# Moving part of the modulation rows' products from VectorE to GpSimd and ScalarE in a two-layer diffusion trunk

## The chip, the cores and the metric

The kernel runs on one core of a Trainium2 chip. Five engines take part, each with its own instruction queue served in order: TensorE (PE in the profile, with PEld for its weight loads), VectorE (DVE), ScalarE (ACT), GpSimd (POOL) and SyncE (SP), from which nearly all transfers are issued. The metric is the device time of one execution in microseconds.

## The reference

The trunk has two layers over 640 tokens (128 of context, 512 latent) of width 2048, all in float32. A layer is a modulated RMS norm, a wide input projection into mixer branches, the mixers, a SiLU gate and an output projection with a gated residual:

```python
shift, scale, gate = modulation(c_ctx, ada_w[l], ada_b[l])     # silu(cond) @ w + b, split in 3
h = rms_norm(x, norm_g[l]) * (1.0 + scale) + shift
...                                                            # y = mixer(h) * silu(gate path)
x = x + gate * (y @ w_out[l])
```

Context tokens use `c_ctx`, latent tokens `c`; so every modulation vector exists twice, once per condition. Layer 0 mixes with windowed attention and gated linear attention (GLA), layer 1 with neighbourhood attention and a spatial-gating MLP. The part that matters here is `modulation`: for each of the 6144 outputs of a layer and each of the two conditions, a dot product over 2048 inputs. In the kernel most of these are not matrix products on TensorE, but products of weight rows with the condition row.

## The kernel before, in words

Features lie on partitions: the activations are 16 tiles of 128 features by 640 tokens. TensorE multiplies in three passes, each operand being split into a high and a low part (`whi`, `wlo` for weights, `acth`, `actl` for activations); ScalarE copies the high part of a weight unit (128 x 512 as a rule), GpSimd subtracts it to get the low part.

The whole order of work is written by a planner at build time. `Pace` keeps a clock for each engine (`t["v"]` VectorE, `t["a"]` ScalarE, `t["g"]` GpSimd), adds a modelled cost to it for each instruction, and knows when a tile will be ready; `self.now` is TensorE's clock. After a few matrix products `tick` is called: it lets the tasks of the main work go on (`tasks`), as long as VectorE and ScalarE are not over `cap` ahead of `now`, and then up to four steps of one low-priority task, `self.low`, but only while `t["v"]` is at most `now + room`. `rooms` gives this threshold: its first value from the end of the start to the second half of the attention (`spill_y`), its third from there, its second from `open_g0` on. `need(flag)` moves the planned clock on, without matrix products of the main line, until a flag is set. `until(tile)` lets a task wait until the plan has a tile ready.

The low-priority task is that of the modulation rows, `ada_task`. It runs three jobs in one chain: `b0` (6 tiles of 128 outputs, a correction of the first gate chunks by the shift), `g0` (16 tiles, layer 0's gate) and `1` (32 tiles, layer 1's shift and scale); later a fourth, `g1`, in narrower pieces. A job goes over the 2048 inputs in four quarters of `PIECE` = 512. At the beginning of a quarter it loads both condition rows, spread over all 128 partitions, and ScalarE copies them into PSUM banks 6 and 7. Then for each tile it loads a 128 x 512 piece of weights into one of four slots of `adas`, and VectorE forms two products with sum (`tensor_tensor_reduce`), one for each condition: a pair.

```python
acc = self.part[name][:, f + k, c : c + 1]
nc.vector.tensor_tensor_reduce(
    junk[:, : bank[c].shape[1]], raw[:, k, :], bank[c], 1.0, acc if q else 0.0, ALU.mult, ALU.add, acc
)
yield pace
```

Each such product is two records in the profile, `CUSTOM_DVE_ANT_0` and a read of the accumulator. The result of job `1` is awaited with `need("ada_1")` ahead of the handover to layer 1; shift and scale are formed from it by `fin_scale` and `shift1`.

The start (`start`) loads inputs, weights for layer 0's scale (24 tiles by TensorE, in `tiles`) and does six first chunks in windows, as activation tiles come in. Beside it runs `shifts` as the low task: the same kind of products for 8 tiles of layer 0's shift, in a ring of `NRAW` pieces. There the two condition rows are not loaded 128-fold: a load of 2 x 512 is split into `chi` and `clo`, and four matrix products with `one` spread them into PSUM banks 2 and 3, in each quarter.

After the start come the GLA heads, the attention heads, then `open_g0`, which is called when the last attention head is done (flag `ya7`): it closes the pool of `YB` and opens the buffers for layer 0's output and layer 1.

## Time and profile before

| what | value |
|---|---|
| median of three runs | 2125.49 us (2121.93 to 2128.29) |
| profiled execution | 2125.07 us |
| its span | 2123.3 us |
| TensorE busy | 2060.7 us (97%) |
| VectorE busy | 1385.2 us (65%) |
| ScalarE busy | 999.3 us (47%) |
| GpSimd busy | 1151.8 us (54%) |
| granted TensorE clock | 0.993 |

In the profile an instruction is named by its line (most have L213, where a helper records each operation, L386 for matrix products, L420 for loads), its engine, its operation, the tile it writes and those that it reads. `adas<-adas,bank,part` is a row product of job `1`, `partg` belongs to `g0` and `g1`, `partb` to `b0`, `raw` and `sh` to the products of the start. Of a group the count, the busy time and the mean of one in ns are given, then the idle time of the engine just ahead of it with what ended it. A view of windows gives busy microseconds of each engine in each stretch, with the granted clock, the share of busy transfer engines and GB/s at the end. A view of one tile gives minimum, median and maximum in ns, and the start of the first and of the last. A line of the waits gives the total, the count and the longest; a line of the timeline the start, the duration and, in brackets, the idle time before it.

### The profile page before, as it was taken

Reading aid. Unit: us, or ns where it says so; the run is one execution under the profiler, and the core shown is the slowest. Engines: PE = TensorE matmul, PEld = TensorE weight load, DVE = VectorE, ACT = ScalarE, POOL = GpSimd, SP = SyncE. Lnnn points to the kernel's source line nnn. Section 1 sums busy time; section 2 is a strip of 40 time slices with the busy share of each in tenths; the row PEclk is TensorE's granted clock in tenths of the full one; section 3 lists DMA queues with packets and bytes.
Section 4 is the critical chain, followed back from the end, with each engine's and each line's share of the span. In section 5 each row is a group of like instructions: output and inputs, shape, how many; then the busy total and the mean of one; then the engine's idle time right before and its main releaser. Section 6 shows DMA issues by size and latency. Waiting matters only on the chain. (4 is left out here: it accounts for less than half of the span.)

```text
span 2123.3 us, 40020 instructions
## 1 busy us (share of the span) xinstructions
PE 2060.7 (97%) x14361; PEld 2007.1 (95%) x14361; DVE 1385.2 (65%) x3260; ACT 999.3 (47%) x2244; POOL 1151.8 (54%) x969
## 2 busy tenths in 40 slices
PE   7999999998999999999999999999999999999996
PEld 6899999998999999999989999999999999999995
DVE  5868777777565664989766878787454444465335
ACT  4424464443555565543464434445444544454433
POOL 4423343333323333788565656555555577668882
PEclk9999999999999999999999999999999999999998
DMA  9956343335454444576734455444222344354327
GB/s 364 377 188 202 116 136 105 114 125 178 148 189 149 139 138 143 179 239 227 248 131 105 130 166 158 139 137 154 89 81 94 107 136 131 124 202 132 127 95 248
DMA packets 192263, 339.13 MB, mean 160 GB/s; under 512 B 20824, under 2 KB 70072, under 8 KB 192064
## 3 DMA queue, kind: packets, MB, share of 16 engines
q1 hardware_dynamic: 190592, 335.02, 47.6%
q8 instruction: 112, 1.84, 0.3%
q10 hardware_dynamic: 1472, 1.56, 0.2%
q14 instruction: 87, 0.71, 0.1%
HBM read 302.00 MB, written 31.88 MB: 157 GB/s over the span
## 5 line engine op out<-in xcount | busy, mean ns | idle before, releaser
L386 PE MATMUL bank<-acth,whi 128*128 128x320 f32 (+2 forms) x3320 | 1022.9, 319 | 18.0 <-ACT bc L213 5.4
L386 PE MATMUL bank<-actl,whi 128*128 128x320 f32 (+2 forms) x3320 | 995.9, 311 | 3.5 <-POOL actl L213 1.7
L386 PE MATMUL bank<-acth,wlo 128*128 128x320 f32 (+2 forms) x3320 | 995.7, 311 | 3.4 <-POOL wlo L213 3.3
L213 POOL TENSOR_TENSOR wlo<-wraw,whi 128x512 fp32r<-128x512 f32 (+1 forms) x452 | 576.2, 1287 | 626.1 <-ACT whi L213 561.4
L386 PEld LDWEIGHTS bank<-acth,whi 128*128 128x128 f32 (+1 forms) x3320 | 618.6, 189 | 28.5 <-ACT bc L213 6.2
L386 PEld LDWEIGHTS bank<-actl,whi 128*128 128x128 f32 (+1 forms) x3320 | 618.4, 189 | 7.1 <-POOL actl L213 2.7
L386 PEld LDWEIGHTS bank<-acth,wlo 128*128 128x128 f32 (+1 forms) x3320 | 618.5, 189 | 5.0 <-POOL wlo L213 5.0
L213 POOL TENSOR_TENSOR wlo<-rs,whi 128x384 fp32r<-128x384 f32 x370 | 406.1, 1117 | 179.5 <-ACT whi L213 143.2
L213 ACT ACTIVATE whi<-wraw 128x512 fp32r<-128x512 f32 (+1 forms) x460 | 263.5, 588 | 138.3 <-PE bank L386 80.6
L386 PE MATMUL bank<-eh,whi 128*128 128x322 f32 (+1 forms) x666 | 209.3, 314 | 0.3 <-ACT whi L213 0.3
L386 PE MATMUL bank<-eh,wlo 128*128 128x322 f32 (+1 forms) x666 | 207.1, 311 | 1.8 <-POOL wlo L213 1.8
L386 PE MATMUL bank<-el,whi 128*128 128x322 f32 (+1 forms) x666 | 206.9, 311 | 0.0
L213 ACT ACTIVATE whi<-rs 128x384 fp32r<-128x384 f32 x370 | 181.4, 514 | 47.1 <-PE bank L386 40.1
L213 DVE CUSTOM_DVE_ANT_0 adas<-adas,bank,partg 128x256 bf16<-128x256 f32 (+1 forms) x320 | 178.5, 558 | 14.4 <-DMA adas<-ada_g 6.4
L213 DVE TENSOR_TENSOR wraw<-rs 128x768 f32<-128x768 f32 x74 | 98.3, 1329 | 122.2 <-POOL wlo L213 51.7
L213 DVE CUSTOM_DVE_ANT_0 adas<-adas,bank,part 128x512 bf16<-128x512 f32 x192 | 143.0, 745 | 15.3 <-DMA adas<-ada 10.6
L213 ACT ACTIVATE arena<-arena,bc 128x512 f32<-128x512 f32 (+4 forms) x211 | 106.3, 528 | 90.3 <-DVE arena L213 87.3
L386 PEld LDWEIGHTS bank<-eh,wlo 128*128 128x128 f32 x666 | 125.5, 188 | 2.7 <-POOL wlo L213 2.5
L386 PEld LDWEIGHTS bank<-eh,whi 128*128 128x128 f32 x666 | 125.7, 189 | 0.6 <-ACT whi L213 0.6
L386 PEld LDWEIGHTS bank<-el,whi 128*128 128x128 f32 x666 | 125.8, 189 | 0.0
L213 POOL TENSOR_TENSOR arena<-arena 128x320 f32<-128x320 f32 (+1 forms) x66 | 70.6, 1069 | 76.5 <-ACT arena L213 65.7
L213 ACT ACTIVATE arena<-Y 128x320 f32<-128x320 f32 (+1 forms) x76 | 38.9, 512 | 151.3 <-DVE Y L213 128.1
(210 smaller groups left out, 2316.1 us busy)
## 6 DMA issues: line engine op xcount, KB each, us to landing
wraw<-w_even SPq DMA_DIRECT2D x176, 256.0 KB, 3.3
adas<-ada_g SPq DMA_DIRECT2D x128, 256.0 KB, 3.6
adas<-ada SPq DMA_DIRECT2D x128, 256.0 KB, 3.6
rs<-w_odd SPq DMA_DIRECT2D x50, 384.0 KB, 3.3
wraw<-w_odd SPq DMA_DIRECT2D x74, 256.0 KB, 3.4
wraw<-w_out SPq DMA_DIRECT2D x64, 256.0 KB, 3.8
rs<-w_odd SPq DMA_DIRECT2D x50, 256.0 KB, 3.6
Y<-ada SPq DMA_DIRECT2D x24, 512.0 KB, 7.1
```

Source lines behind the costliest of these rows:

```text
L213: return f(*args, **kw)
L386: self.nc.tensor.matmul(out, lhsT, rhs, start=start, stop=stop, **kw)
```

## The change

Three things change.

First, the products for the second condition (c = 1) may be taken off VectorE. `offload` gives one to GpSimd as a plain elementwise product into one of two buffers (`prods`), if fewer than two are open and GpSimd's planned clock is not past `now` (`mixed` is 0). `collect`, called ahead of each product, lets ScalarE sum a finished buffer into a column of `psum`. GpSimd reads the condition row from a copy in SBUF, `mixrow`. At the end of a job, VectorE adds the four quarters' columns to the job's result. From `open_g0` on `prods` is empty, and all products are VectorE's again. The same is done in the start.

Second, the first threshold `rooms[0]` goes from 0.3 to 0.0: from the start's end to `spill_y`, a step of the row task is taken only when VectorE's planned clock is not past `now`.

Third, in the start the condition rows come 128-fold by transfer, one row at a time, and ScalarE copies them into the banks; the split and the four matrix products per quarter go. The ring of pieces shrinks from six to five, and `junk` and `crow` move into free parts of `adas`.

```diff
+        self.mixrow = [self.t(yb, [128, PIECE], "mixrow", bufs=2) for _ in range(2)]
+        self.prods = [self.t(yb, [128, PIECE], "prod", bufs=2) for _ in range(2)]
+        self.made, self.nprod = [], 0
+        self.psum = self.P([128, 4, 32], "psum")
+        for x in self.part.values():
+            nc.gpsimd.memset(x, 0.0)
...
-    cap, hold = 2.0, 99.0
-    lags0, room0, rows_at, pace0, NRAW, NRING = (0.2,) * 5, 1.2, 20.0, 0.4, 6, 6
+    cap, hold, mixed = 2.0, 99.0, 0.0
+    lags0, room0, rows_at, pace0, NRAW, NRING = (0.2,) * 5, 1.2, 20.0, 0.4, 5, 6
-    rooms, calms, lags = (0.3, 1.5, 0.9), (3.0, 3.0), (3.0, 3.0, 2.0, 1.0, 0.4)
+    rooms, calms, lags = (0.0, 1.5, 0.9), (3.0, 3.0), (3.0, 3.0, 2.0, 1.0, 0.4)
...
     def ada_task(self, jobs):
...
-            if isinstance(job, list):
-                for k, b in enumerate(job):
+            if len(job) == 2:
+                for k, b in enumerate(job[0]):
                     nc.scalar.activation(b, raw[:, k, :], AF.Copy)
+                    if self.prods and b is self.banks[7]:
+                        nc.scalar.activation(self.mixrow[job[1] % 2], raw[:, k, :], AF.Copy)
+                        if job[1] == 0:
+                            nc.gpsimd.memset(self.psum, 0.0)
...
+                    self.collect()
+                    if c == m == 1 and self.offload(raw[:, 0, :], self.mixrow[q % 2], self.psum[:, q, f : f + 1]):
+                        yield
+                        continue
                     nc.vector.tensor_tensor_reduce(
-                        junk[:, : bank[c].shape[1]], raw[:, k, :], bank[c], 1.0, acc if q else 0.0, ALU.mult, ALU.add, acc
+                        junk[:, : bank[c].shape[1]], raw[:, k, :], bank[c], 1.0,
+                        acc if (f + k, c) in begun else 0.0, ALU.mult, ALU.add, acc
                     )
...
             if last:
+                while self.made:
+                    self.collect()
+                    yield
+                begun.clear()
+                if m == 1:
+                    for q in range(4):
+                        acc = self.part[name][:, :, 1]
+                        nc.vector.tensor_tensor(acc, acc, self.psum[:, q, 0 : acc.shape[1]], ALU.add)
...
+    def offload(self, raw, row, acc):
+        if len(self.made) >= len(self.prods) or self.pace.t["g"] > self.now + self.mixed:
+            return False
+        x = self.prods[self.nprod % len(self.prods)]
+        self.nprod += 1
+        self.nc.gpsimd.tensor_tensor(x, raw, row, ALU.mult)
+        self.made.append((x, acc))
+        return True
+
+    def collect(self, force=False):
+        while self.made and (force or self.left(self.made[0][0]) <= 0.0):
+            x, acc = self.made.pop(0)
+            self.nc.scalar.activation(x, x, AF.Copy, accum_out=acc)
...
             def shifts():
...
-                junk = self.t(su, [128, PIECE // 2], "junk").bitcast(BF16)
-                one = self.t(su, [2, 2, 128], "one", F32R)
-                hi, lo = (self.t(su, [2, PIECE], x, F32R) for x in ("chi", "clo"))
-                nc.vector.tensor_copy(one, self.ident[0:2, 0:2, None].to_broadcast([2, 2, 128]))
+                junk = self.adas[:, 1472 : 1472 + PIECE // 2].bitcast(BF16)
...
-                    todo += [(None, d["crow_s"][:, cs]), *((f, d["ada_s0"][f, :, cs]) for f in range(NB))]
+                    todo += [(-c, d["crow_s"][2 - c : 3 - c, cs].partition_broadcast(128)) for c in (2, 1)]
+                    todo += [(f, d["ada_s0"][f, :, cs]) for f in range(NB)]
...
-                    if f is None:
-                        raw = raw[0:2, :]
-                        yield from self.until(raw)
-                        nc.scalar.activation(hi, raw, AF.Copy)
-                        nc.vector.tensor_tensor(lo, raw, hi.bitcast(F32), ALU.subtract)
+                    if f < 0:
+                        nc.scalar.activation(pc[f + 2], raw, AF.Copy)
+                        if f == -1:
+                            nc.scalar.activation(self.mixrow[q % 2], raw, AF.Copy)
                         load(i + len(raws) - 1)
-                        yield from self.until(hi, lo)
-                        for c, p in enumerate(pc):
-                            self.mm(p, one[:, c, :], hi, stop=False)
-                            self.mm(p, one[:, c, :], lo, start=False)
                         continue
...
         def open_g0():
             self.need("ya7")
+            self.collect(True)
+            self.prods = []
```

In `shifts` the products get the same `collect` and `offload` calls, and the same four additions behind them.

## The prediction

> **What bounds the kernel now.** I read the page's first part first, to see which engine is full.

> ```profile
> span 2123.3 us, 40020 instructions
> PE 2060.7 (97%) x14361; PEld 2007.1 (95%) x14361; DVE 1385.2 (65%) x3260; ACT 999.3 (47%) x2244; POOL 1151.8 (54%) x969
> ```

> TensorE is the bound; it is idle for 2123.3 - 2060.7 = 62.6 us, and no work moved between the other three engines can gain more than the part of that idle time which the moved work causes. So I next asked for the busy time of each engine by stage, cut at 148 (the start ends), 228 and 533 (the loads of `ada_g0` and `ada_1` begin), 790 (the moved work is nearly over) and 1041 (the last row product of layer 1 ends).

> ```profile
> core 0: us, PE busy (x) PEld busy (x) DVE busy (x) ACT busy (x) POOL busy (x), PEclk, DMA share, GB/s
> 0.00:28.00 28.00, 17.81 (x216) 13.94 (x216) 7.67 (x14) 13.14 (x28) 11.66 (x16) 1.00 0.91 354
> 28.00:110.00 82.00, 75.27 (x926) 65.70 (x927) 67.98 (x139) 39.72 (x86) 38.93 (x27) 1.00 0.98 378
> 110.00:148.00 38.00, 38.00 (x276) 36.41 (x276) 29.68 (x81) 7.30 (x15) 10.64 (x10) 1.00 0.45 151
> 148.00:228.00 80.00, 80.00 (x547) 79.99 (x546) 61.76 (x127) 36.46 (x70) 31.52 (x25) 1.00 0.58 187
> 228.00:533.00 305.00, 296.31 (x2029) 291.16 (x2028) 220.52 (x432) 137.53 (x261) 120.08 (x80) 0.99 0.40 131
> 533.00:790.00 257.00, 254.63 (x1692) 244.53 (x1691) 157.20 (x479) 147.47 (x373) 84.07 (x64) 1.00 0.46 152
> 790.00:900.00 110.00, 107.50 (x718) 105.25 (x717) 75.18 (x156) 59.43 (x130) 61.23 (x49) 1.00 0.48 157
> 900.00:1041.00 141.00, 135.42 (x909) 133.99 (x908) 122.83 (x281) 53.28 (x120) 112.82 (x104) 0.99 0.69 231
> ```

> The second number is TensorE's busy time. From 148 to 790 it loses 11.1 us (8.7 + 2.4), from 790 to 1041 8.1 us, from 28 to 110 6.7 us, from 110 to 148 nothing. In 28 to 110 the DMA engines are at 0.98: that stage is fed by transfers. Now what ended the losses, by the waits of TensorE for 148 to 790:

> ```profile
> PE bank L386 <- ACT bc L213: 5.4, 3, 3.5
> PE bank L386 <- DVE arena L213: 2.5, 5, 1.1
> PE bank L391 <- ACT arena L213: 2.4, 3, 1.1
> PE bank L391 <- DVE Y L213: 0.8, 1, 0.8
> ```

> These are releases of PSUM banks by the evacuation: VectorE multiplies, ScalarE copies the bias columns after it. Row products sit in VectorE's queue between such steps. The clearest case is the last of them, in order of time:

> ```profile
> 1035.56 0.31 PE L386 MATMUL bank<-acth,whi 128*128 128x320 f32 x1
> 1036.14 0.75 DVE L213 CUSTOM_DVE_ANT_0 adas<-adas,bank,part 128x512 bf16<-128x512 f32 x1 [4.54 <-DMA adas<-ada]
> 1037.60 0.89 DVE L213 TENSOR_TENSOR bank<-bank,sums 128x320 f32<-128x320 f32 x2
> 1038.53 1.14 DVE L213 SCALAR_TENSOR_TENSOR Y<-bank,G,arena 128x128 f32<-128x128 f32 x3
> 1039.26 0.42 PE L386 MATMUL bank<-acth,whi 128*128 128x320 f32 x1 [3.39 <-DVE Y L213]
> ```

> VectorE stood 4.54 us for a piece of layer 1's rows, the evacuation stood behind it, and TensorE lost 3.39 us. The code has a `need("ada_1")` here; the rows were barely in time.

> **The change part by part.** Durations of what goes and comes, by form:

> ```profile
> L213 DVE CUSTOM_DVE_ANT_0 adas<-adas,bank,part 128x512 bf16<-128x512 f32 x192 | 143.0, 745 | 15.3 <-DMA adas<-ada 10.6
> L213 DVE DVE_READ_ACCUMULATOR2_ANT part<- 128x1 f32 x256 | 21.1, 83 | 0.0
> L213 POOL TENSOR_TENSOR wlo<-wraw,whi 128x512 fp32r<-128x512 f32 x300 | 407.3, 1363 | 530.8 <-ACT whi L213 477.8 <-PE bank L386 33.5 <-DMA adas<-ada 4.8
> L213 ACT ACTIVATE whi<-wraw 128x512 fp32r<-128x512 f32 x308 | 190.3, 624 | 127.1 <-PE bank L386 71.6 <-issue 20.0 <-POOL wlo L213 14.4
> L213 ACT ACTIVATION_READ_ACCUMULATOR arena<-arena,nm 128x1 f32 x40 | 7.5, 187 | 0.0
> ```

> One moved product takes 745 + 83 = 0.83 us off VectorE, and puts 1.36 us on GpSimd (the nearest GpSimd row of two 128x512 operands) and 624 + 187 = 0.81 us on ScalarE.

> *Start: rows by DMA.* Out go four sets of four TensorE matmuls, and the copy and subtraction that feed them; in come eight broadcasts of 256 KB for four small loads of 4 KB.

> ```profile
> 40.83 0.49 PE L386 MATMUL bank<-chi,one 2*128 2x512 f32 x1
> 41.95 0.41 PE L386 MATMUL bank<-acth,suhi 128*128 128x320 f32 x1
> L420 SPq DMA_DIRECT2D raw<-crow_s x4: 250/254/313, 27.6 to 118.8; - x4
> L213 ACT ACTIVATE adas<-Y x15: 720/737/742, 14.7 to 83.6; 128x640 f32<-128x640 f32 x15
> adas<-crow_s SPq DMA_DIRECT2D x24, 256.0 KB, 4.7
> ```

> A set takes 41.95 - 40.83 = 1.12 us of TensorE, four sets 4.5 us. The bytes are 8 x 256 - 4 x 4 = 2032 KB, 2.08 MB; at 378 GB/s that is 5.5 us of a full transfer stage. Only what comes ahead of the last activation tile can starve TensorE; that tile's input is squared at 83.6 (third row), and the four loads of rows stand between 27.6 and 118.8, so that two of them come before it: half, 2.7 us. Ends: 0 (covered by windows in hand) and 5.5; I take 2.5, since transfers are full there and TensorE is not. ScalarE gets eight bank copies and four copies into `mixrow` for four old ones, 8 x 0.62 = 5.0 us (the 624 ns row), beside its 39.7 of 82 busy: nothing on the path; without that slack the activation tiles would come later by as much. On SP four more issues, 4 x 0.25 us, in a queue that waits for buffers anyway. Fewer VectorE products help after 110, where TensorE has no idle time: nothing. The ring falls from 6 to 5 slots, two of which now hold rows at each quarter: nothing while VectorE, not the ring, sets the pace; if it did, one landing of 4.7 us per quarter. Sum of the start: -4.5 + 2.5 = -2.0 us; range -4.5 to +3.

> *148 to 790: the split of products and the new threshold.* Both act only here: `prods` is emptied at `open_g0`. How many move? `offload` asks that GpSimd's planned clock is not ahead of TensorE's. A weight unit keeps that clock ahead from its split until its GpSimd subtraction ends, about 0.6 + 1.36 us plus the lead of the plan (0.4 to 1 us), say 2.6 us. From 148 to 790 the trace has one such unit in 4.5 us:

> ```profile
> L213 POOL TENSOR_TENSOR wlo<-wraw,whi x144: 1268/1293/2477, 148.7 to 793.4; 128x512 fp32r<-128x512 f32 x144
> ```

> (793.4 - 148.7) / 144 = 4.5. So GpSimd counts as free 1 - 2.6 / 4.5 = 0.42 of the time, less its other work; I take 0.35 of the second products. Tile loads give the number of pairs:

> ```profile
> L420 SPq DMA_DIRECT2D adas<-ada x128: 327/338/1718, 533.4 to 1031.0; - x128
> L420 SPq DMA_DIRECT2D adas<-gateT x24: 327/333/639, 149.7 to 206.2; - x24
> 768.79 0.33 SPq L420 DMA_DIRECT2D adas<-crow_s  x1
> 819.13 1.75 SPq L420 DMA_DIRECT2D arena<-yT_dram  x4
> ```

> The third quarter's rows of job 1 load at 768.8, so half of that job is done by 790; the handover's loads at 819 stand just behind `open_g0`, so the last 25 us of offloading I leave out. b0 has 24 pairs, g0 64 and that half 64: 152 pairs, 0.35 x 152 = 53 products. VectorE loses 53 x 0.83 = 44 us of its 439 (61.8 + 220.5 + 157.2), GpSimd gains 72 on 236, ScalarE 43 on 321. The threshold falling from 0.3 to 0 keeps a 0.83 us product from being queued in front of work up to 0.3 us off; it takes no work away. Of the 11.1 us that TensorE waits, nearly all for VectorE and what follows it, I take a third away: -3.5 (ends 0 and -8). What is new behind waits: a sum on ScalarE waits for its product, and behind it stand weight copies and bias columns; a subtraction on GpSimd waits up to 1.36 us behind a product. Weights are split several units ahead (no `POOL wlo` row in that list), so I take +2 (ends 0 and +14, see rivals). Net -1.5.

> What may take this back:

> ```profile
> 1075.79 4.03 POOL L213 TENSOR_TENSOR wlo<-wraw,whi 128x512 fp32r<-128x512 f32 x3
> 1078.71 1.46 DVE L213 TENSOR_TENSOR arena<-arena 128x320 f32<-128x320 f32 x1
> 1084.07 0.49 DVE L213 TENSOR_TENSOR arena<-arena 128x320 f32<-128x320 f32 x1
> L213 DVE CUSTOM_DVE_ANT_0 adas<-adas,bank,part x192: 731/748/750, 662.2 to 1040.4; 128x512 bf16<-128x512 f32 x192
> ```

> One VectorE form, with both inputs in SBUF, takes 1.46 us beside a GpSimd subtraction and 0.49 alone; the row product, with one input in PSUM, takes 731 to 750 ns whatever GpSimd does. So moving it turns an operation that GpSimd does not touch into one that stretches others. [...]

> *790 to 1041: rows sooner.* What the pairs took: g0 (533.4 - 228) / 64 = 4.8 us, job 1 (1041 - 533.4) / 128 = 4.0. A pair needed two idle gaps of VectorE; with 0.35 moved it needs 1.65, and I put the lower threshold at 8% fewer gaps: rate x 0.92 x 2 / 1.65 = 1.12. To 790 that brings 152 x 0.12 = 18 pairs more, and at 4.0 us each the rows end some 70 us before 1041. Then the 3.39 us wait goes, and about 1 of the other 2.2 lost in 900 to 1041 (5.6 in all): -4.4. What is late next there is the weight split on GpSimd. The four new additions at the job's end are of this kind:

> ```profile
> 1041.04 0.17 DVE L213 TENSOR_TENSOR A<-part,b 128x16 f32<-128x16 f32 x1
> ```

> With rows in time they are off the path; with rows late they cost 4 x 0.17 = 0.7 us.

> *Without cost:* zeroing of small tiles on GpSimd, ten or so row copies on ScalarE (0.62 us each, spread over 640 us), the moved scratch areas.

> Sum: -2.0 - 1.5 - 4.4 = -7.9 us. The profiled execution took 2125.07 us, its span 2123.3 and 1.8 around it, 0.4 under the median 2125.49. Forecast 2125.1 - 7.9 = 2117 us; its own range, from the ends above, 2108 to 2121.

> **Rivals.** *Hidden (within 0.3%).* If GpSimd's planned clock is nearly always ahead, few products move, and the change does not do what it says: the middle stage and the rows stay as they are, and only the start's -2 counts: 2123. For it: two thirds of a unit's 4.5 us are closed already by my own count. Against: GpSimd is busy 236 of 642 us there.

> *Locked (within 0.3%).* Beside each product one VectorE operation is stretched by 1.46 - 0.49 = 0.97 us: 53 x 0.97 = 51 us against the 44 saved. VectorE gains nothing, rows end no sooner: 2123, with the +2 of new waits 2125. Against: row products are a good part of VectorE's work there and are not stretched, so not every product meets a victim.

> *Rows late (slower).* The threshold of 0 alone makes gaps rarer. It decides where the share of lost gaps exceeds half the share of moved products (0.175 at 0.35). With a quarter of the gaps lost and one product in ten moved, the rate is 0.75 x 2 / 1.9 = 0.79: 152 x 0.21 = 32 pairs are missing at 790, and at `need("ada_1")` TensorE is held while VectorE makes them, 2 x 0.83 = 1.66 us each, 53 us; if half is made up in gaps before, 26 us: 2125 - 2 + 26 = 2149. Against: job 1, most of it under thresholds of 0.9 and 1.5, took 4.0 us a pair, g0 under 0.3 took 4.8; the threshold weighs little.

> *Queues coupled (slower).* GpSimd and ScalarE serve in order. If a fifth of the products' 72 us reaches TensorE through weight splits and bank releases, that is 14 us in place of my 2: 2129; with the rows no sooner, 2134. For it: ScalarE releases 7.8 of the 11.1 us. Against: no wait for `wlo` from 148 to 790.

> **How the numbers follow.** Chances: forecast 0.45, hidden 0.14, locked 0.14, rows late 0.13, queues coupled 0.14. A change of this kernel can be told from none beyond about 0.3%, 6.4 us at the median: faster under 2119.1, slower over 2131.9. The forecast lies under in four fifths of its cases (0.36), and hidden and locked, where the start gives its full -4.5 and more, add 0.07: faster 0.43. Same: 0.09 of the forecast, 0.19 of hidden and locked, 0.05 of coupled: 0.33. Slower: the rest, 0.24. The range leaves out most of rows late and the forecast's lower tail: 2107 to 2139.

> **What would show it.** TensorE's row for 28 to 110 and the end of the start stage near 146 (start right); groups `prod` on GpSimd and ScalarE with about 53 in 148 to 790 besides those of the start; last load of job 1's rows well before 1031; no wait of 3 us at `need("ada_1")`. The prediction is wrong if job 1's rows end later than 1041, if `POOL wlo` or `ACT prod` shows among TensorE's waits with over 5 us, or if far fewer than 53 products move.

## The result, and the profile after

The changed kernel takes 2119.88 us in the median of 16 runs (2117.51 to 2123.52), beside 2125.63 us (2121.93 to 2128.29) of the kernel before in as many: 5.7 us less, where 2117 was forecast. The ratio of the means is 0.9976, with a 95% interval of 0.9969 to 0.9984: by it 5.1 us less. The first part of its page:

```profile
span 2117.1 us, 40263 instructions
PE 2058.0 (97%) x14345; PEld 2003.7 (95%) x14345; DVE 1320.0 (62%) x3063; ACT 1071.2 (51%) x2471; POOL 1285.1 (61%) x1082
```

VectorE lost 65 us, GpSimd won 133 and ScalarE 72: the move took place. The span is 6.2 us shorter: TensorE's idle time fell from 62.6 to 59.1 us, its busy time by 2.7. The stages of the prediction from 28 to 790, busy time of each engine with the granted clock:

```profile
core 0: us, PE busy (x) PEld busy (x) DVE busy (x) ACT busy (x) POOL busy (x), PEclk, DMA share, GB/s
28.00:110.00 82.00, 77.39 (x942) 68.33 (x941) 61.93 (x115) 47.66 (x109) 52.57 (x38) 0.98 1.02 392
110.00:148.00 38.00, 36.08 (x269) 35.10 (x269) 22.77 (x67) 16.31 (x39) 22.61 (x20) 1.00 0.62 196
148.00:228.00 80.00, 76.82 (x514) 74.92 (x513) 53.25 (x107) 47.42 (x103) 47.85 (x37) 1.00 0.59 183
228.00:533.00 305.00, 300.80 (x2071) 295.88 (x2070) 207.48 (x391) 160.43 (x332) 163.03 (x114) 1.00 0.45 139
533.00:790.00 257.00, 254.00 (x1682) 242.94 (x1681) 143.02 (x428) 167.24 (x445) 128.62 (x99) 1.00 0.50 154
```

Against the kernel before, TensorE is idle 3.2 us in 148 to 228, where it was never idle, and 4.2 us in 228 to 533, where it was idle 8.7. Since the two kernels do the same work at different moments, a stage's sum can mislead. I therefore counted, in windows from a moment to the end, how many matrix products TensorE had left, and looked up when another kernel has as many left. At 228 us the kernel before has 12,402 left; the changed kernel has 12,402 left at 229.5, so there it is 1.5 us behind. The order of TensorE's own work differs between kernels, so the count says how much is left, not which. The table gives this lead (minus) or lag (plus) in us, for each kernel of this study against the profiled execution of the kernel before.

| at, in the kernel before | 145 | 160 | 228 | 475 | 533 | 790 | 1016 | 1060 | 1120 | 2090 |
|---|---|---|---|---|---|---|---|---|---|---|
| changed kernel | -3.2 | -3.4 | 1.5 | 2.0 | -4.5 | -3.1 | -2.2 | -4.3 | -5.5 | -6.0 |
| x1_start | -1.8 | -0.1 | 4.5 | 3.4 | -2.5 | 0.5 | 1.6 | 9.2 | 8.8 | 8.5 |
| x3_nooffload | 1.4 | 3.6 | 4.0 | 2.9 | -1.5 | 0.8 | 3.1 | 18.8 | 18.0 | 16.4 |
| x2_room03 | -2.5 | -2.5 | 4.0 | 11.0 | 10.3 | 11.9 | 17.7 | 12.8 | 12.0 | 12.0 |
| x4_nob0 | -1.6 | -1.8 | -1.8 | 3.2 | -2.9 | -1.5 | 3.2 | -1.6 | -2.3 | -4.0 |
| y1_start_room3 | 0.3 | 2.2 | 3.0 | 1.7 | -3.8 | -1.8 | 8.8 | 3.8 | 4.1 | 3.4 |
| y2_sum1 | -2.3 | -2.3 | 2.0 | 3.7 | -2.6 | -2.2 | 6.0 | 1.5 | 0.7 | 0.2 |
| y3_lag | -1.6 | -1.8 | 3.4 | 2.9 | 2.6 | 4.4 | 6.5 | 3.2 | 2.5 | 1.3 |
| y5_before_room3 | 2.4 | 2.3 | 2.4 | 2.4 | 1.1 | 2.0 | 9.5 | 6.8 | 6.2 | 4.8 |
| z_before_room05 | 0.1 | 0.1 | 0.3 | -1.0 | -2.8 | 1.2 | 1.3 | 0.0 | 0.2 | -0.2 |
| z_after_room05 | -2.4 | -2.5 | 3.1 | 4.9 | 3.9 | 4.2 | 4.6 | 1.8 | 1.1 | -0.3 |
| z_before_room13 | 0.8 | 0.8 | 1.3 | 1.4 | 1.2 | 1.6 | 3.5 | 2.0 | 2.0 | -0.1 |
| z_after_room13 | -1.0 | -1.2 | 3.4 | 4.4 | -2.6 | 0.4 | 0.0 | -1.3 | -1.8 | -3.2 |

Each row is one execution, and its grain is coarse. x1_start and x3_nooffload run the same program up to 160 and differ there by 3.7 us; x1_start and y1_start_room3 run the same one up to 790, and from 160 to 228 the first loses 4.6 us, behind one wait of 2.08 us for `bc` with a drop of the clock to 0.50, the second 0.8. So a step between two columns counts here only where several executions agree on it.

For the changed kernel the row reads: 3.2 us won in the start, 4.9 lost in the stage of job `b0` (160 to 228), 6.5 won at the end of GLA (475 to 533), 2.3 lost from there to 1016, some 2 won at `need("ada_1")`, 1.2 in the handover behind it. z_after_room13, the same program up to 790, agrees in the first three (-1.2 at 160, then 4.6 lost and 7.0 won). Its waits of TensorE over the whole span, the costliest behind the transfers of the start (3.4 us for `arena` from VectorE, ahead of the last line, are left out):

```profile
PE bank L393 <- POOL wlo L213: 6.2, 8, 1.4
PE bank L398 <- ACT arena L213: 4.8, 8, 1.2
PE bank L393 <- ACT adas L213: 4.4, 3, 1.9
PE bank L393 <- ACT bc L213: 3.3, 4, 1.6
```

The groups that were to show the steps, of the changed kernel: products on GpSimd in the row jobs and in the start, the row products that stayed on VectorE in job 1, and the loads of that job's pieces.

```profile
L213 POOL TENSOR_TENSOR prod<-adas,mixrow x85: 1260/1292/1978, 151.6 to 809.9; 128x512 f32<-128x512 f32 x85
L213 POOL TENSOR_TENSOR prod<-raw,mixrow x19: 1277/1292/1535, 42.2 to 134.0; 128x512 f32<-128x512 f32 x19
L213 DVE CUSTOM_DVE_ANT_0 adas<-adas,bank,part x151: 728/748/751, 637.6 to 1017.5; 128x512 bf16<-128x512 f32 x151
L427 SPq DMA_DIRECT2D adas<-ada x128: 327/328/1311, 519.7 to 1003.3; - x128
```

85 products moved beside the row jobs, not 53. The last load of job 1 stands at 1003.3 (before 1031.0), its last product at 1017.5 (before 1040.4).

**Where 6.5 us at the end of GLA come from.** In the kernel before, in order of time, the step that opens the last chain of a head and the end of that chain:

```profile
480.81 1.03 DVE L213 TENSOR_SCALAR arena<-bank 128x320 f32<-128x320 f32 x2 [0.80 <-PE bank L386]
487.60 0.48 DVE L213 TENSOR_TENSOR arena<-bank,rstd 128x320 f32<-128x320 f32 x1
488.17 0.17 ACT L213 ACTIVATE bc<-bank 128x2 f32<-128x2 f32 x1 [4.79 <-DVE arena L213]
488.40 0.41 PE L386 MATMUL bank<-acth,whi 128*128 128x320 f32 x1 [3.53 <-ACT bc L213]
```

and in the changed kernel the same steps:

```profile
477.75 1.03 DVE L213 TENSOR_SCALAR arena<-bank 128x320 f32<-128x320 f32 x2 [1.19 <-PE bank L393]
484.72 0.48 DVE L213 TENSOR_TENSOR arena<-bank,rstd 128x320 f32<-128x320 f32 x1
485.24 0.17 ACT L213 ACTIVATE bc<-bank 128x2 f32<-128x2 f32 x1 [2.95 <-DVE arena L213]
```

This is a chain of VectorE (the closing steps of a GLA head) that frees a PSUM bank through the small copy `bc`. It ends 2.9 us sooner, and TensorE comes 2 us later, so its 3.53 us wait is gone. The chain is no shorter: from its opening step to `bc` it takes 7.4 us before and 7.5 now, and VectorE stands idle ahead of that step in both, 0.80 and 1.19 us, for products of TensorE. So it isn't a freer VectorE at this point that took the wait away, but the order of TensorE's own work, with the chain's products set earlier among the others; what made the plan set them so was not traced. Nor does this wait give lost time back by itself: y5_before_room3 and z_before_room13, whose program is that of the kernel before up to 790, come here 2.4 and 1.4 us later and wait the same 3.53 us. The rest of the gain is in two gaps behind it and in the clock: in windows of 2 us, the kernel before 516 to 526.

```profile
516.00:518.00 2.00, 1.04 (x8) 0.78 (x7) 1.96 (x6) 0.22 (x2) 0.00 (x0) 1.00 0.77 178
518.00:520.00 2.00, 1.25 (x7) 0.97 (x7) 1.96 (x6) 0.75 (x2) 0.00 (x0) 1.00 0.61 189
520.00:522.00 2.00, 1.62 (x8) 1.62 (x9) 1.89 (x7) 1.62 (x4) 1.07 (x1) 0.69 0.72 232
522.00:524.00 2.00, 2.00 (x9) 2.00 (x9) 1.93 (x5) 0.63 (x1) 0.90 (x2) 0.50 0.76 203
524.00:526.00 2.00, 2.00 (x15) 2.00 (x14) 1.89 (x7) 0.00 (x0) 0.59 (x1) 0.96 0.32 103
```

After two gaps, of 0.96 us and of 1.13 us (which the window's end at 520 cuts into 0.75 and 0.38), the granted clock (third number from the end) falls to a half; what TensorE loses by it is 0.31 x 1.62 + 0.5 x 2 + 0.04 x 2 = 1.6 us on top of the 2.1 us of idleness. In the changed kernel one gap of 0.90 us is left there, and no drop.

**`need("ada_1")`.** The 3.39 us wait and its drop of the clock are gone. In the kernel before (first fence, windows of 2 us) the drop costs 0.1 x 0.74 + 0.5 x 2 + 0.25 x 2 = 1.6 us more; in the changed kernel (second fence, in order of time) another wait stands ahead of the same point.

```profile
1038.00:1040.00 2.00, 0.74 (x4) 0.74 (x5) 1.97 (x6) 0.47 (x1) 0.21 (x1) 0.90 0.14 52
1040.00:1042.00 2.00, 2.00 (x9) 2.00 (x9) 1.93 (x6) 0.99 (x2) 1.42 (x2) 0.50 0.73 230
1042.00:1044.00 2.00, 2.00 (x13) 2.00 (x12) 1.67 (x7) 0.39 (x3) 1.38 (x2) 0.75 1.01 308
```

```profile
1018.32 4.23 DVE L213 TENSOR_TENSOR part<-part,psum 128x32 f32<-128x32 f32 x4
1020.23 3.23 POOL L213 TENSOR_TENSOR wlo<-wraw,whi 128x512 fp32r<-128x512 f32 x3
1022.48 1.02 DVE L213 TENSOR_TENSOR A<-part,b 128x16 f32<-128x16 f32 x1
1023.91 0.48 DVE L213 TENSOR_TENSOR sums<-sums,bank 128x320 f32<-128x320 f32 x1
1024.45 0.41 PE L393 MATMUL bank<-acth,whi 128*128 128x320 f32 x1 [1.59 <-DVE sums L213]
```

The four closing additions take 4.23 us instead of the 0.7 that I set for them: each has both inputs in SBUF and stands beside GpSimd's weight subtractions, and so does the addition behind them (1.02 us). `sums` is behind them in VectorE's queue, and TensorE waits 1.59 us for it.

### The profile page after: what moved, and what is told of

It reads as the page before. It is cut to its first block, busy times and chain, and to the rows that moved or that the text cites. A ratio compares the mean times of both kernels' runs of the same rounds, so it can differ in the third digit from the quotient of the medians.

```text
span 2117.1 us, 40263 instructions
## 1 busy us (share of the span) xinstructions
PE 2058.0 (97%) x14345; PEld 2003.7 (95%) x14345; DVE 1320.0 (62%) x3063; ACT 1071.2 (51%) x2471; POOL 1285.1 (61%) x1082
## 5 line engine op out<-in xcount | busy, mean ns | idle before, releaser
L393 PE MATMUL bank<-acth,whi 128*128 128x320 f32 (+2 forms) x3320 | 1021.5, 318 | 10.6 <-ACT bc L213 2.8
L213 POOL TENSOR_TENSOR wlo<-wraw,whi 128x512 fp32r<-128x512 f32 (+1 forms) x452 | 573.6, 1281 | 412.1 <-ACT whi L213 329.8
L213 POOL TENSOR_TENSOR wlo<-rs,whi 128x384 fp32r<-128x384 f32 x370 | 408.1, 1123 | 183.2 <-ACT whi L213 143.6
L213 ACT ACTIVATE whi<-wraw 128x512 fp32r<-128x512 f32 (+1 forms) x460 | 262.9, 588 | 93.2 <-PE bank L393 60.7
L213 ACT ACTIVATE whi<-rs 128x384 fp32r<-128x384 f32 x370 | 182.0, 514 | 48.5 <-PE bank L393 41.7
L213 DVE TENSOR_TENSOR wraw<-rs 128x768 f32<-128x768 f32 x74 | 98.8, 1335 | 124.7 <-POOL wlo L213 69.9
L213 DVE CUSTOM_DVE_ANT_0 adas<-adas,bank,partg 128x256 bf16<-128x256 f32 (+1 forms) x290 | 156.2, 539 | 12.6 <-DMA adas<-ada_g 5.3
L213 POOL TENSOR_TENSOR prod<-adas,mixrow 128x512 f32<-128x512 f32 x85 | 111.5, 1321 | 70.4 <-ACT prod L213 48.5
L213 ACT ACTIVATE arena<-arena,bc 128x512 f32<-128x512 f32 (+4 forms) x211 | 106.4, 527 | 79.8 <-DVE arena L213 77.0
L213 DVE CUSTOM_DVE_ANT_0 adas<-adas,bank,part 128x512 bf16<-128x512 f32 x151 | 112.4, 744 | 9.8 <-DMA adas<-ada 6.8
L213 ACT ACTIVATE arena<-Y 128x320 f32<-128x320 f32 (+1 forms) x76 | 38.9, 512 | 152.1 <-DVE Y L213 125.9
## 6 DMA issues: line engine op xcount, KB each, us to landing
wraw<-w_even SPq DMA_DIRECT2D x176, 256.0 KB, 3.4
adas<-ada_g SPq DMA_DIRECT2D x128, 256.0 KB, 3.7
adas<-ada SPq DMA_DIRECT2D x128, 256.0 KB, 3.8
wraw<-w_odd SPq DMA_DIRECT2D x74, 256.0 KB, 3.5
wraw<-w_out SPq DMA_DIRECT2D x64, 256.0 KB, 3.9
rs<-w_odd SPq DMA_DIRECT2D x50, 256.0 KB, 3.8
```

The lines of the kernel that those rows point to most:

```text
L213: return f(*args, **kw)
L393: self.nc.tensor.matmul(out, lhsT, rhs, start=start, stop=stop, **kw)
```

## The experiments

Each ratio is to the kernel before on the same chip; all kernels compute the whole reference. The changed kernel was not timed again beside the other runs, whose kernels before came out at 2123.53 to 2125.14 us against 2125.63 beside it, so a difference to the changed kernel is sure to some 2 us.

### The start's part alone (x1_start), and with the threshold 0.0 (x3_nooffload)

x1_start loads the start's rows by transfer, with the ring of 5, but moves no product and keeps the threshold at 0.3; x3_nooffload has the threshold 0.0 as well. The edits against the changed kernel:

```diff
-        self.prods = [self.t(yb, [128, PIECE], "prod", bufs=2) for _ in range(2)]
+        self.prods = []
...
-    rooms, calms, lags = (0.0, 1.5, 0.9), (3.0, 3.0), (3.0, 3.0, 2.0, 1.0, 0.4)    # x1_start only
+    rooms, calms, lags = (0.3, 1.5, 0.9), (3.0, 3.0), (3.0, 3.0, 2.0, 1.0, 0.4)
```

(The row copies into `mixrow` and the closing additions go too.)

> Only the start's part of the change: condition rows by transfer, ring of five pieces; no product moved (the buffers' list is empty), threshold 0.3 as before. If the start's gain is the four sets of matrix products less the transfers, as forecast, and it is carried through to the end: 2 to 4 us faster than before (2122 to 2124). If later stages give it back (a start that ends sooner only waits later for rows): within 1 us of before.

> The change without the moved products: rows by transfer in the start, threshold 0, all products on VectorE. Theory A (the lower threshold alone starves the rows and the moved products make that good): the rows end 20 us or more later than with threshold 0.3, a wait at need(ada_1) of 10 us or more, 2130 to 2150. Theory B (the threshold is nearly neutral for the rows, and it is the threshold that takes the waits at the end of the GLA heads away): no more than 2 us from the whole change, 2118 to 2122.

Measured: x1_start 2132.12 us, ratio 1.003 (1.0018 to 1.0042); x3_nooffload 2139.45 us, ratio 1.0067 (1.0043 to 1.0091). So x1_start is slower than either of its expectations, x3_nooffload is where theory A had it, and neither the start's part nor the threshold is worth anything by itself. The first lines of the waits of x1_start and of x3_nooffload that aren't transfers say why:

```profile
PE bank L393 <- ACT whi L213: 10.4, 2, 9.7
```

```profile
PE bank L393 <- ACT whi L213: 14.7, 1, 14.7
```

These long ones are TensorE at `need("ada_1")`. The last row product of job 1 begins at 1052.4 and at 1061.6, against 1040.4 before, and the table has the loss in one place, 1016 to 1060: 1.6 to 9.2, and 3.1 to 18.8. The start's part sets the rows back on its own: in x1_start the start's second quarter of products begins at 97.3 (before 84.8), the last of the start's products at 145.7 (142.7), `b0`'s last load is at 217.0 (206.2) and job 1's first at 560.4 (533.4; 560.0 and 560.6 in the two other kernels that move nothing). Why the delay grows behind the start was not tested. The threshold takes 9 us more from them up to the last product. In the changed kernel the moved products pay that back. This is the rival "rows late", true in its mechanism, and avoided by the number of products moved.

### The whole change with the old threshold (x2_room03)

```diff
-    rooms, calms, lags = (0.0, 1.5, 0.9), (3.0, 3.0), (3.0, 3.0, 2.0, 1.0, 0.4)
+    rooms, calms, lags = (0.3, 1.5, 0.9), (3.0, 3.0), (3.0, 3.0, 2.0, 1.0, 0.4)
```

> The whole change with the threshold left at 0.3. Theory B (the threshold does the gain between 475 and 533): the gain there, 6.5 us, is gone, 2124 to 2127. Rival C (moved products do it, by taking work off VectorE): the gain stays, 2118 to 2121.

Measured: 2136.82 us, ratio 1.0051 (1.0033 to 1.0069). Its rows are the earliest of all (last product at 984.8), and still it is 17 us slower than the changed kernel. The table has it 11.0 behind at 475 and 17.7 at 1016, and its waits name the chains of VectorE:

```profile
PE bank L393 <- DVE arena L213: 9.2, 8, 3.1
PE bank L393 <- ACT bc L213: 7.8, 5, 3.5
PE bank L398 <- DVE Y L213: 5.9, 1, 5.9
```

The threshold of 0.0 by itself costs 7 us (x1 to x3), with the moved products it gains 17. I read this as VectorE's chains being what counts once products go to GpSimd, with the threshold keeping row products from in front of them; no run shows that by itself. In the longest of these waits, 5.9 us at 388, one row product of 0.74 us stands in the chain, and three of its steps of 128x640 take 1.73 to 1.88 us beside GpSimd's work, some 2.9 us more together than alone (0.82 each).

### No product of job b0 moved (x4_nob0)

```diff
-                    if c == m == 1 and self.offload(...):
+                    if c == m == 1 and name != "b0" and self.offload(...):
```

> The whole change, but no product of job b0 is moved. Theory D (between 160 and 228 TensorE loses 5 us against before because ScalarE and GpSimd stand in order behind loads and products of b0): 3 to 5 us faster than the whole change, 2115 to 2117. If the loss there has another cause (the threshold, or the order of the plan): within 1.5 us of the whole change.

Measured: 2122.77 us, ratio 0.9994 (0.9983 to 1.0004). The stage of `b0` is whole again (-1.6 at 145, -1.8 at 228, against -3.2 and +1.5): the 4.9 us there come from moving that job's products. But the gain of 3 did not reach the end, and the kernel is 2.9 us slower than the changed one where 3 to 5 us less were expected; a new wait of 4.36 us stands in GLA, in order of time:

```profile
370.06 6.99 POOL L213 TENSOR_TENSOR wlo<-wraw,whi 128x512 fp32r<-128x512 f32 x4 [0.54 <-DMA adas<-ada_g]
374.10 1.80 DVE L213 TENSOR_TENSOR arena<-Y 128x640 f32<-128x640 f32 x1
377.01 3.64 POOL L213 TENSOR_TENSOR prod<-adas,mixrow 128x512 f32<-128x512 f32 x2
379.46 1.88 DVE L213 TENSOR_TENSOR Y<-arena 128x640 f32<-128x640 f32 x1
381.39 0.33 PE L398 MATMUL bank<-ident,Y 128*128 128x128 f32 x1 [4.36 <-DVE Y L213]
```

The steps of the GLA chain that take 0.82 to 0.83 us in the median of the kernel before take 1.80 to 1.88 beside GpSimd's subtractions and products, and the products themselves 1.82 each instead of 1.29. That is the rival "locked" at one place: the two steps above take 0.98 and 1.05 us more, where the rival had 0.97 beside each product.

### Rows sooner by a higher threshold: y1_start_room3 and y5_before_room3

Theory: what x1_start lost, and the 3.39 us of the kernel before, is the wait at `need("ada_1")` alone; then a higher threshold from `open_g0` on brings both back. The same edit in x1_start and in the kernel before (there 0.3, 1.5, 0.9 too):

```diff
-    rooms, calms, lags = (0.3, 1.5, 0.9), (3.0, 3.0), (3.0, 3.0, 2.0, 1.0, 0.4)
+    rooms, calms, lags = (0.3, 3.0, 0.9), (3.0, 3.0), (3.0, 3.0, 2.0, 1.0, 0.4)
```

> The start's rows by DMA alone (nothing moved to GpSimd, threshold 0.3 up to the end of layer 0's attention, as in x1_start), with the threshold after that raised from 1.5 to 3.0, so that the row products go into more gaps of VectorE. Theory 'rows late': x1_start's 9 us came from layer 1's rows being 12 us late at the point that needs them and from nothing else. Then the last row product falls from 1052 to before 1040, the wait of 9.7 us behind it goes, and the time is 2120 to 2124 (x1_start 2132 less 8 to 12), with the start's gain left over. Rival 'gaps cost': products queued further ahead of VectorE's due work delay TensorE's evacuations between 790 and 1040 by as much as the wait was worth: 2129 to 2134.

> The kernel before, with one number changed: the threshold from the end of layer 0's attention on is 3.0 for 1.5. If the wait of 3.39 us for layer 1's rows in the kernel before is just a matter of rows that are late by a few us, it goes here too and the time is 2121 to 2123, so that some 3 of the change's 5.7 us were to be had without moving any product. If products queued further ahead cost as much as the wait, the time stays within 1 us of 2125.5; and if the wait is not made by the rows, it stays in the trace.

Measured: y1_start_room3 2130.74 us, ratio 1.0025 (1.0014 to 1.0037); y5_before_room3 2132.29 us, ratio 1.0033 (1.0022 to 1.0044). y5_before_room3 was expected within 1 us of the kernel before at the worst. In both the wait at `need("ada_1")` is gone (last row product at 1038.7 and 1032.5), and in both the price is paid elsewhere: y1_start_room3 goes from -1.8 at 790 to +8.8 at 1016, y5_before_room3 from 2.0 to 9.5. y1_start_room3 in order of time:

```profile
899.31 0.74 DVE L213 CUSTOM_DVE_ANT_0 adas<-adas,bank,part 128x512 bf16<-128x512 f32 x1
900.09 0.75 DVE L213 CUSTOM_DVE_ANT_0 adas<-adas,bank,part 128x512 bf16<-128x512 f32 x1
900.77 0.49 DVE L213 TENSOR_TENSOR actl<-bank,acth 128x320 fp32r<-128x320 f32 x1
901.31 0.63 PE L393 MATMUL bank<-actl,whi 128*128 128x320 f32 x1 [0.75 <-DVE actl L213]
```

Two row products stand ahead of the step that makes `actl`, for which TensorE waits; from 895 to 902 this gives gaps of 0.68, 0.97, 1.08 and 0.75 us, and the clock is at 0.50 up to 907. So "gaps cost" holds, not "rows late" alone. With the rows made by VectorE alone, TensorE pays either at `need("ada_1")` or in the gaps before it. The moved products leave fewer products for the same gaps: in the seven kernels that move them the last row product begins at 984.8 to 1019.7, and TensorE has no wait of 3 us at this point.

### The closing additions as one sum (y2_sum1)

```diff
-                    for q in range(4):
-                        acc = self.part[name][:, :, 1]
-                        nc.vector.tensor_tensor(acc, acc, self.psum[:, q, 0 : acc.shape[1]], ALU.add)
+                    acc = self.part[name][:, :, 1]
+                    tot = self.adas[:, 4 * PIECE : 4 * PIECE + acc.shape[1]]
+                    nc.vector.tensor_reduce(tot, self.psum[:, :, 0 : acc.shape[1]].rearrange("p q f -> p f q"), AX.X, ALU.add)
+                    nc.vector.tensor_tensor(acc, acc, tot, ALU.add)
```

> The whole change, but the four final additions of 128x16 are one reduction over the quarters and one addition. If the four additions of 0.93 to 1.22 us (4.2 us together) are what TensorE's 1.59 us wait for the scales at 1024 hangs on, two instructions take some 2 us, the wait goes, and the time is 1 to 2 us under the changed kernel: 2118 to 2119. If the wait hangs on the last row product itself or on the weight split beside it, the time stays within 0.7 us of 2120. Should the cost be one per instruction with two operands in SBUF beside GpSimd's work, the reduction (one operand) takes well under 0.9 us and only the addition is near 1 us.

Measured: 2125.2 us, ratio 0.9996 (0.9986 to 1.0006); the expected gain is missing in the total, and there in its place. The reduction and what follows:

```profile
L213 DVE TENSOR_REDUCE adas<-psum x3: 198/275/375, 226.4 to 1016.1; 128x6 f32<-128x24 f32 x1, 128x16 f32<-128x64 f32 x1, 128x32 f32<-128x128 f32 x1
1016.47 0.79 DVE L213 TENSOR_TENSOR part<-part,adas 128x32 f32<-128x32 f32 x1
```

0.375 + 0.79 us stand for 4.23, and the 1.59 us wait for `sums` is gone; the addition with two inputs in SBUF is still near 0.8 us. What took it back is at 813 and 848 us, at the attention's end, where another order came out: a wait of 2.73 us for `arena` from ScalarE, whose cause I did not trace, and one behind a step that fell beside GpSimd's work. First y2_sum1, then the same step in the changed kernel:

```profile
846.07 1.88 DVE L213 TENSOR_TENSOR Y<-Y,arena 128x320 f32<-128x320 f32 x1 [3.32 <-ACT arena L213]
848.41 0.41 PE L393 MATMUL bank<-acth,whi 128*128 128x320 f32 x1 [2.69 <-DVE arena L213]
```

```profile
841.37 0.49 DVE L213 TENSOR_TENSOR Y<-Y,arena 128x320 f32<-128x320 f32 x1 [2.39 <-ACT arena L213]
```

This second wait is 2.69 us, with a drop of the clock to 0.50 behind it; from 790 to 1016 this kernel loses 8.2 us against 0.9 of the changed kernel, though no edit aims at that stage.

### Sums given to ScalarE later (y3_lag)

```diff
-        while self.made and (force or self.left(self.made[0][0]) <= 0.0):
+        while self.made and (force or self.pace.ready("t", [], [self.pace.span(self.made[0][0])]) + 1.5 <= self.now):
```

> The whole change, but the sum of a moved product is given to ScalarE only 1.5 us after the product's planned end. Theory 'queues coupled in b0's stage': ScalarE stands 15 us behind products from 148 to 816, bank copies stand behind it, and TensorE loses about 5 us between 160 and 228. Then ScalarE's idle time behind products falls under 5 us, TensorE keeps 2 to 4 us of the lost 5, and the time is 2116 to 2118, if the products' two buffers, held longer, don't cut the number moved by more than a tenth. Rival: the loss in b0's stage comes from GpSimd (weights split late behind products) and from TensorE's new wait for bias columns behind bank copies that wait for their rows' landing; then ScalarE's waits go and the time stays at 2119 to 2121.

Measured: 2124.9 us, ratio 0.9997 (0.9985 to 1.001). ScalarE's waits for products from 148 to 816, in the changed kernel and in y3_lag:

```profile
ACT prod L213 <- POOL prod L213: 15.1, 8, 5.1
```

```profile
ACT prod L213 <- POOL prod L213: 4.9, 3, 2.2
```

The waits fell as meant, and `b0`'s stage still loses 5.2 us (-1.8 to +3.4). So the sums that wait for their products aren't what costs TensorE there; that theory fell, and the time is in neither of the ranges expected. Why moving `b0`'s products costs 5 us is open: most of the 3.2 us of idleness follows ScalarE (`bc` 1.6, `arena` 1.3), and ScalarE's bank copies wait 6.9 us for their rows' transfers in that stage, against 3.1 before, but I took neither away.

### Small moves in both kernels (four z kernels)

y2_sum1 and y3_lag changed hardly anything and lost 5 us. So the last four kernels ask how much of the 5.7 us belongs to the order of work that happened to come out. The first threshold is raised by 0.05, or the second lowered from 1.5 to 1.3, once in each kernel:

```diff
-    rooms, calms, lags = (0.3, 1.5, 0.9), (3.0, 3.0), (3.0, 3.0, 2.0, 1.0, 0.4)     # before
+    rooms, calms, lags = (0.35, 1.5, 0.9), (3.0, 3.0), (3.0, 3.0, 2.0, 1.0, 0.4)    # z_before_room05
+    rooms, calms, lags = (0.3, 1.3, 0.9), (3.0, 3.0), (3.0, 3.0, 2.0, 1.0, 0.4)     # z_before_room13
-    rooms, calms, lags = (0.0, 1.5, 0.9), (3.0, 3.0), (3.0, 3.0, 2.0, 1.0, 0.4)     # changed
+    rooms, calms, lags = (0.05, 1.5, 0.9), (3.0, 3.0), (3.0, 3.0, 2.0, 1.0, 0.4)    # z_after_room05
+    rooms, calms, lags = (0.0, 1.3, 0.9), (3.0, 3.0), (3.0, 3.0, 2.0, 1.0, 0.4)     # z_after_room13
```

> The kernel before with one planning number moved a little: the threshold of layer 0's stage 0.35 for 0.3. No work is added or taken away; some row products stand in other gaps of VectorE. Theory 'one order of work': the measured gain of 5.7 us belongs to the particular order that came out, and orders that differ by a few products spread by several us, so this kernel lies anywhere from 2121 to 2132, and about as often under as over the kernel before. Theory 'the change itself': small moves of a threshold cost under 1.5 us, 2124 to 2127.

> The changed kernel with the same small move, 0.05 for 0.0. Theory 'one order of work': 2119 to 2127, with no fixed distance to its counterpart of the kernel before. Theory 'the change itself': 2118.5 to 2121.5, and 4 to 7.5 us under its counterpart. Theory 'threshold protects the evacuations' (0.3 cost 17 us): a sixth of that, 2122 to 2124.

> The kernel before with the threshold after layer 0's attention 1.3 for 1.5, so nothing differs up to 790 us. Theory 'one order of work': 2121 to 2132. Theory 'rows late': layer 1's rows, which TensorE awaited for 3.39 us already, come later still, and the wait at that point grows: 2126 to 2131. Theory 'the change itself' (small moves cost nothing): 2124 to 2127.

> The changed kernel with the same move, 1.3 for 1.5. Its rows are 23 us ahead of the kernel before, so 'rows late' expects no wait for them here and 2119 to 2121, while its counterpart loses. 'One order of work' expects 2119 to 2127.

| edit | kernel before: ratio (interval) | changed kernel: ratio (interval) |
|---|---|---|
| none | 1 | 0.9976 (0.9969 to 0.9984) |
| first threshold + 0.05 | 1.0006 (0.9997 to 1.0016) | 1.0006 (0.9997 to 1.0016) |
| second threshold 1.3 | 1.0004 (0.9994 to 1.0013) | 0.9987 (0.9978 to 0.9996) |

In us between the medians: 0.5 of the gain is left in the first pair (2125.75 and 2125.27; the ratios are equal, so no gain can be told there), 3.2 in the second (2125.08 and 2121.85; the two intervals just touch). The kernel before hardly reacts to either edit, the changed kernel by 2 to 6 us, more than "the change itself" allowed. z_after_room05 shows where: it is at +4.9 at 475 and +3.9 at 533, so that the gain of 6.5 at the end of GLA is only 1.0 there; TensorE waits 3.8 us there for `arena` from ScalarE, and the clock drops to 0.50 at 523. Three orders of the changed kernel thus lie 0.5 to 5.7 us under their counterparts. Its rows are ahead in all of them (last product at 1017.5, 1016.1 and 1019.7, against 1040.4, 1040.5 and 1045.5).

## Why the prediction was right or wrong

**Start, -2.0.** Right in size, not in the step behind it. At 160, with the start over, the seven kernels that have the whole start lead by 1.2 to 3.4 us, 2.2 in the mean. But the forecast had this from the matrix products saved (-4.5) less the transfers (+2.5), and the three kernels that have these two and move no product don't lead: x1_start is 0.1 ahead, y1_start_room3 and x3_nooffload 2.2 and 3.6 behind, as the other kernels with the start of before are (0.1 to 2.3 behind). So the gain came only with the products moved in the start, for which the forecast had "nothing". What I also missed is that the start's part delays the row work ("nothing while VectorE, not the ring, sets the pace"): VectorE waits 4.4 us for the start's pieces in x1_start, in the kernel before it never does, and job 1's loads begin 27 us later, which without moved products costs 8 us at `need("ada_1")`.

**The share of products moved, 0.35 of 152 = 53.** Mis-sized: 85 moved beside the row jobs, of 24 + 64 + (809.9 - 519.7) / ((1003.3 - 519.7) / 128) = 165 pairs, a half; 83 of them before 790. Which factor in my count of GpSimd's closed time was off was not measured.

**148 to 790, waits relieved -3.5, new ones +2.** Both mis-sized, and they don't just add. New waits cost 4.9 us (4.3 to 5.6 in the other four kernels that move `b0`'s products under a threshold of 0.0 or 0.05), all in `b0`'s stage, not spread; the relief was 6.5 us, all at the end of GLA: 3.53 us of wait, 1.2 of other gaps and a drop of the clock. Net from 145 to 790 it was +0.1 where I had -1.5; TensorE's waits in that stretch fell only from 11.1 to 10.0 us. The step that failed is "a third of the 11.1 us": waits don't shrink in proportion to the moved work, single ones go or stay as a whole. Nor is moved work needed for this one, or enough: x1_start and y1_start_room3 show the same gain from 475 to 533 (5.9 and 5.5) without any moved product and under the old threshold, y3_lag almost none (0.3) with 80, and x2_room03 still has the wait of 3.53 us with 102.

**Threshold, "8% fewer gaps", "weighs little".** Wrong. It weighs 7 us without moved products and 17 with them, in opposite directions (x1 to x3; x2 to the changed kernel). Where its worth comes from stays open: what stands behind a product in VectorE's queue is my reading, not a result.

**Rows 70 us sooner, wait of 3.39 gone, -4.4.** The wait went, and with it 1.6 us of lost clock that the sum had not counted; the rows came 23 us sooner (last product), a third of the forecast. With the old threshold they came 56 us sooner (x2_room03), so the threshold took 33 of the missing 47. From 790 to 1060 only 1.2 us were won, not 4.4: the weight split on GpSimd rose from 1.8 to 3.5 us of waits between 905 and 1045, as "what is late next" said, and the closing additions added 1.59.

**"Four additions, 0.17 us each".** Wrong by six times: 4.23 us for four, since the row I took (128x16, 0.17 at 1041.04) had no GpSimd work beside it; the same kind of step just behind it, at 1041.24, stood beside GpSimd and took 0.90. y2_sum1 shows the wait going with them.

**The rivals.** *Hidden*: no, 104 products moved. *Locked*: its price was for a victim at each product, 51 us; the operations that grew most from 148 to 816 (`arena<-arena` of 128x512 and of 128x640) grew by 6.5 us together. But single victims decide single waits: 4.36 us in x4_nob0, 2.69 in y2_sum1. *Rows late*: its wait is what x1_start and x3_nooffload lost, 9.7 and 14.7 us; the changed kernel stays clear of it by the moved half. *Queues coupled*: 5 us in `b0`'s stage, but not by sums that wait (y3_lag).

**Signs and sums.** One sign of being wrong came up by its letter: `POOL wlo` stands among TensorE's waits with 6.2 us. The kernel before has 5.1 over its whole span already, so the sign was badly set; from 148 to 790 there is none in either. Two sums don't come out: the upper end of the start, from -4.5 and 5.5, is +1, not +3, and the upper end of the range, 2121, leaves out that end and the +14 of new waits.

The forecast's range (2108 to 2121 by its own terms) holds the 2119.9, with every term off in its size or in the step behind it and the errors cancelling; that the total fits is luck. By the table's row the start gave 3.2 us, 145 to 790 nothing, 790 to 1060 1.2, and 1.7 came behind 1060, where the forecast had no term. What the runs leave of "faster" is smaller: the change brings the rows sooner in every order tried, and the changed kernel lies 0.5 (not told from none), 3.2 and 5.7 us under its counterparts.

## What to carry to other kernels

When low-priority work is moved off an engine, the gain is a few whole waits, not a share of all waits: find the points where the bound engine waits for a chain that it doesn't set itself, and ask of each whether it goes. Time lost ahead of such a point isn't given back there of itself: executions of one program came to the end of GLA up to 2.4 us apart and waited the same 3.53 us. Before a gain of 0.3% in a planned order of work is credited to a change, move an unrelated number of the plan a little in both kernels: if the gain changes by as much as its size, it belongs partly to the order.

## What the runs showed of the hardware

```profile
483.21:486.63 3.42, 1.66 (x12) 1.00 0.05 17
486.63:490.04 3.41, 1.64 (x11) 1.00 0.00 0
490.04:493.45 3.41, 3.41 (x25) 1.00 0.00 0
```

The same wait in the same program is followed by one slow window in y5_before_room3 and by two in z_before_room13. The 1.59 us at 1024 in the changed kernel falls on two windows, without a drop; the 2.46 us at the same point in z_after_room13 falls in one, with a drop. A slow window cost up to 1.7 us (3.41 us at 0.50); by that, an estimate, a wait of 2 us costs 2 to 3.7. In sum (busy time x what is missing from a clock of 1) the slow windows cost 6.8 us in the kernel before, 5.1 in the changed kernel, 12.2 in x1_start and 12.1 in x2_room03; so 1.7 of the 6.2 us between the two spans are clock. The window ahead of the slow one at 520.76 in the kernel before, one of the 13, has 1.76 us of idleness in two pieces.

**Tiny additions took up to 1.22 us.** 128x32 with two inputs in SBUF took 0.93 to 1.22 us beside GpSimd's subtractions; the same kind of addition for job `b0` (128x6) took 0.16 to 0.17 us, and 128x16 between 0.18 and 0.47, the longest where a subtraction was still running. 128x32 without GpSimd's work beside it was not measured.
